# Front of a gated short-convolution layer: three of sixteen first sums on the matrix engine, a finer load, and three splits behind the front

## The chip, the cores and the metric

The kernel runs on one core of a Trainium2 chip. The core's engines work beside each other, each through its own list of instructions in a fixed order: TensorE (PE, matrix products; PEld is its loading of weights), VectorE (DVE), ScalarE (ACT), GpSimd (POOL) and SyncE (SP), which here issues nearly all transfers from the chip's memory. The metric is the device time of one execution in microseconds (us); lower is better.

## The reference, cut to what matters

One layer: a root-mean-square norm of x (256 tokens of 2048 features), a modulation whose shift, scale and gate come from a vector c through `ada_w` (2048 x 6144), a projection by `w_in` (2048 x 16384) into four quarters of 4096, a causal convolution of width 3 and two gatings, a projection back by `w_out` (4096 x 2048), the gated residual and a last norm, all in float32.

```python
h = rmsnorm(x, norm_g)
mod = einsum('bd,df->bf', silu(c), ada_w) + ada_b
shift, scale, gate = split(mod, 3)
h = h * (1.0 + scale) + shift
b_gate, c_gate, v, g = split(einsum('bsd,de->bse', h, w_in), 4)
u = causal_depthwise_conv(c_gate * v, conv_w)
y = einsum('bse,ed->bsd', b_gate * u * silu(g), w_out)
out = rmsnorm(x + gate * y, final_g)
```

## The kernel before, in words

**Products.** A float32 product is made of three faster ones: each weight tile is split into a rounded part `hi` (ScalarE, line 338) and the rest `lo` (VectorE, line 339), h likewise into `hh_` and `hl_`, and TensorE adds hi·hh, hi·hl and lo·hh (line 466). The raw weight tiles (`raw0`, `raw_s`) rotate through three buffers, `hi` and `lo` through three each.

**The front** (lines 195 to 403) is written out by hand, and `in_order` keeps it in that order on every engine. SyncE loads x, then the columns of `ada_w` for the first two 128-feature blocks of shift and scale (tiles `at0`, the k-th holding rows k of the 16 blocks of 128 rows), then the first weights `raw0`. The tiles `at0` borrow the buffers of `lo` and `hi` in turn, three of each. The first sums, silu(c) times these columns over the 16 blocks k, are made in two ways: for the k in `ON_PE` TensorE multiplies the columns directly (`sum0_of`, line 350); for the others VectorE accumulates into `gv0` (lines 362 and 364), and at the end TensorE adds up `gv0` over the partitions into the same bank (line 387). From the sums come `scale` and `shift`, and `features(k)` (lines 326 to 332) gives `hh_` on ScalarE and `hl_` on VectorE for the first two blocks k = 0, 1. Between these, TensorE turns x in four steps (`turn_x`, line 306) once ScalarE has scaled it (`scaled_x`), and makes idle products (`idle`, line 253), whose numbers stand in `IDLE`.

**Behind the front** a planner (`plan`) lays out steps: a step is a pair of chunks (of 512 columns each), a quarter, and a range of blocks k for which h is ready. The first steps have the two blocks k = 0, 1 alone: 24 products from `raw0`, 24 from a half load `raw_s`, then 48 for every whole load. Between the loads go pieces of the next modulation sums (`ada_piece`: two transfers of 256 KB to a tile `at`, four buffers; VectorE adds them into `gv`, lines 446 and 448). When a pair of blocks is summed, TensorE turns the sums (`tp_g`, line 455), ScalarE adds them up, and `features` gives the next two blocks of h. What lies behind the front is put in order by a scheduler that fills each engine's list with what it thinks ready, so a waiting instruction of the front can be passed by later work; on the engine itself the list is then followed strictly. Later stages (`mm_b`, line 466 too, and the projection back, lines 670 to 672) are not touched.

Of the kernel before, what the change touches and what calls it, by code (L numbers as in the profile page):

```python
# [11 lines left out]
ALU = mybir.AluOpType  # L12
# [116 lines left out]
def short_conv_layer(ctx: ExitStack, tc: tile.TileContext, x, c, norm_g, ada_w, ada_b, w_in, conv_w, w_out, final_g, out):  # L129
    nc = tc.nc  # L130
# [59 lines left out]
    ended = {}  # L190
# [5 lines left out]
    rows2 = const.tile([96, P], F32, tag="rows2", name="rows2")  # L196
    HX = D // 2
    GIVE = 300
    IDLE = (20, 8, 28, 2, 6, 4, 12, 8)
    xt = [[slot([P, HX], f"x{t}{dh}") for dh in range(2)] for t in range(TT)]  # L200
    for t in range(TT):
        for dh in range(2):
# [8 lines left out]
    adas = ada_w[0].rearrange("(k p) (s f) -> p k s f", p=P, s=3)  # L211
    NK0 = ADA[0]
    first_ada = []
    for n, (j, kk) in enumerate(((0, 4), (4, 4), (8, 4), (12, 2), (14, 1), (15, 1))):
        at = wpool.tile([P, SLOT], F32, tag=("lo", "hi")[n % 2], name="at0", bufs=3)[:, : kk * 2 * NK0 * P]
        at = at.rearrange("p (k s f) -> p k s f", k=kk, s=2)
        if n == 0:
            wpool.tile([P, 32], F32, tag="line3", name="line3", bufs=1)
        for s in range(2):
            nc.sync.dma_start(at[:, :, s, :], adas[:, j : j + kk, s, 0 : NK0 * P])  # L220
        first_ada.extend(at[:, i] for i in range(kk))
# [118 lines left out]
        return hi, lo  # L340


    ON_PE = (3, 7, 11, 13)
    sums0 = psum.tile([P, 512], F32, tag="sm", name="sum0", bufs=2)
    gv0 = adap.tile([P, 2, 2 * P], F32, tag="gv", name="gv0")[:, :, 0 : NK0 * P]

# [19 lines left out]
    scaled_x(1)  # L366
    turn_x(turned[0], 0)
    nc.scalar.copy(xs[0], turned[0])
    sum0_of(0)
    scaled_x(2)  # L370
    turn_x(turned[1], 1)
    nc.scalar.copy(xs[1], turned[1])
    idle(3, turned[2])
    sum0_of(1)
    idle(4, turned[2])
    scaled_x(3)
    turn_x(turned[2], 2)
    nc.scalar.copy(xs[2], turned[2])
    turned.append(psum.tile([P, CT, T], F32, tag="mm", name="tp_x"))
    idle(5, turned[3])  # L380
    sum0_of(2)
    turn_x(turned[3], 3)
    nc.scalar.copy(xs[3], turned[3])
    sum0_of(3)
    tp_idle = psum.tile([P, CT, T], F32, tag="mm", name="tp_idle")
    idle(6, tp_idle)
    sum0(None, gv0, ones[:, 0:1])

    sums_shift, sums_scale = sums0[:, 0:NK0], sums0[:, NK0 : 2 * NK0]
    ks = slice(0, NK0)  # L390
    nc.vector.tensor_tensor(out=scale[:, ks], in0=sums_scale, in1=b_scale1[:, ks], op=ALU.add)
    nc.vector.tensor_tensor(out=scale[:, ks], in0=scale[:, ks], in1=gT[:, ks], op=ALU.mult)
    nc.vector.tensor_tensor(out=shift[:, ks], in0=sums_shift, in1=b_shift[:, ks], op=ALU.add)
    hi0 = wpool.tile([P, SLOT], F32R, tag="hi", name="hi", bufs=3)
    lo0 = wpool.tile([P, SLOT], F32R, tag="lo", name="lo", bufs=3)
    w = CT * P
# [2 lines left out]
    for k in range(NK0):  # L399
        c = slice(k * w, (k + 1) * w)  # L400
        nc.vector.tensor_tensor(out=lo0[:, c], in0=raw0[:, c], in1=hi0[:, c].bitcast(F32), op=ALU.subtract)
        features(k)
    idle(7, tp_idle)
    pinned.close()
    pieces0 = [(hi0, lo0)]

# [87 lines left out]
    def keep(ch, q, k0, bank, seed=False):  # L494
# [4 lines left out]
        else:  # L499
            nc.vector.tensor_tensor(out=acc[ch, q], in0=bank, in1=acc[ch, q], op=ALU.add)  # L500

    def parts(chs, q, k0, k1, seeds, between):

        w = len(chs) * CT * P
# [16 lines left out]
        for s0, some in zip(range(k0, k1, step), between):  # L521
            sk = min(step, k1 - s0)
            n = sk * w
            raw = raw_tile("raw_s")
            nc.sync.dma_start(
                raw[:, :n].rearrange("p (k f) -> p k f", k=sk),
                w_in[0, s0 * P : (s0 + sk) * P, col : col + w].rearrange("(k p) f -> p k f", p=P),
            )
            hi, lo = split(raw, n)
            for piece in some:  # L530
                ada_piece(*piece)
            for j, (bank, seed) in enumerate(zip(banks, seeds)):
                if first == 0:
                    opening_products(bank, hi, lo, w, j * CT * P, s0, sk, k1)
                else:
                    for i in range(sk):
                        chunk_products(bank, hi, lo, i * w + j * CT * P, s0 + i, first, k1, seed)
# [236 lines left out]
```

## Time and profile before

| | |
|---|---|
| median of three runs | 913.68 us (913.65 to 915.89) |
| the profiled execution | 913.47 us, its span 911.7 us |
| TensorE busy in the span | 898.6 us (99%) |
| VectorE, ScalarE busy | 628.8 us (69%), 451.7 us (50%) |
| read from memory | 224.49 MB |

A row of the timeline gives the start, the duration, the engine (with q: its issuing part), the line, the operation, what is written and read, how many such instructions follow each other, and in brackets how long the engine sat idle before and what ended that. 913.47 less 911.7 leaves 1.8 us around the span, which is taken as fixed.

### The profile page before, as it was taken

Reading aid. Unit: us, or ns where it says so; the run is one execution under the profiler, and the core shown is the slowest. Engines: PE = TensorE matmul, PEld = TensorE weight load, DVE = VectorE, ACT = ScalarE, POOL = GpSimd, SP = SyncE. Lnnn points to the kernel's source line nnn. Section 1 sums busy time; section 2 is a strip of 40 time slices with the busy share of each in tenths; the row PEclk is TensorE's granted clock in tenths of the full one; section 3 lists DMA queues with packets and bytes.
Section 4 is the critical chain, followed back from the end, with each engine's and each line's share of the span. In section 5 each row is a group of like instructions: output and inputs, shape, how many; then the busy total and the mean of one; then the engine's idle time right before and its main releaser. Section 6 shows DMA issues by size and latency. Waiting matters only on the chain.

```text
span 911.7 us, 16332 instructions
## 1 busy us (share of the span) xinstructions
PE 898.6 (99%) x7111; PEld 866.5 (95%) x7111; DVE 628.8 (69%) x605; ACT 451.7 (50%) x427; POOL 0.7 (0%) x6
## 2 busy tenths in 40 slices
PE   8999999999999999999999999999999999999997
PEld 7899999999999999999999999999999988888885
DVE  4888989999988999985555455545455544555882
ACT  6678876544545755554333443334433333443333
POOL 0000000000000000000000000000000000000000
PEclk9999999999999999999999999999999999999999
DMA  9999999999898778867666666666666496665542
GB/s 305 375 384 372 321 361 349 329 362 351 286 350 308 239 246 280 281 225 223 198 188 187 193 200 202 190 186 191 200 192 201 141 346 213 198 202 195 185 139 92
DMA packets 146791, 227.64 MB, mean 250 GB/s; under 512 B 5360, under 2 KB 103840, under 8 KB 146336
## 3 DMA queue, kind: packets, MB, share of 16 engines
q1 hardware_dynamic: 146480, 226.51, 74.0%
q8 instruction: 55, 0.90, 0.4%
q14 instruction: 16, 0.13, 0.0%
q10 hardware_dynamic: 240, 0.09, 0.0%
HBM read 224.49 MB, written 2.10 MB: 249 GB/s over the span
## 4 chain that ended last, share of the span: by engine, by line
PE 95%; DMA 3%; DVE 1%; ACT 0%; SPq 0%; issue 0%; ACTq 0%; DVEq 0%
PE mm_b L466 38%; PE mm_s L466 37%; PE mm_o L671 6%; PE mm_o L670 6%; PE mm_o L672 6%; DMA raw_s<-in_sc_w_in_dram 1%; DMA at<-in_ada_w_dram 1%; DMA x<-in_x_dram 1%; DVE gv L364 1%; PE tp_g L455 0%; ACT hi L338 0%; PE ps_gate L609 0%; SPq L220 0%; DVE lo L339 0%; PE sum L350 0%; SPq L203 0%
## 5 line engine op out<-in xcount | busy, mean ns | idle before, releaser
L466 PE MATMUL mm_b<-hT,hi 128*128 128x256 f32 x2048 | 348.4, 276 | 0.0
L466 PE MATMUL mm_s<-hT,hi 128*128 128x256 f32 x2048 | 336.6, 277 | 1.6 <-ACT hi L338 1.0
L466 PEld LDWEIGHTS mm_b<-hT,hi 128*128 128x128 f32 x2048 | 308.4, 188 | 0.0
L466 PEld LDWEIGHTS mm_s<-hT,hi 128*128 128x128 f32 x2048 | 299.4, 188 | 2.5 <-ACT hi L338 1.2
L466 PE MATMUL mm_b<-hT,lo 128*128 128x256 f32 x1024 | 282.6, 276 | 0.0
L466 PE MATMUL mm_s<-hT,lo 128*128 128x256 f32 x1024 | 262.1, 276 | 0.0
L339 DVE TENSOR_TENSOR lo<-raw,hi 128x2048 fp32r<-128x2048 f32 x64 | 146.7, 2291 | 128.2 <-ACT hi L338 128.2
L338 ACT CAST hi<-raw 128x2048 fp32r<-128x2048 f32 x64 | 122.5, 1913 | 196.3 <-PE mm_b L466 149.0
L466 PEld LDWEIGHTS mm_b<-hT,lo 128*128 128x128 f32 x1024 | 192.2, 188 | 0.1
L466 PEld LDWEIGHTS mm_s<-hT,lo 128*128 128x128 f32 x1024 | 182.8, 188 | 0.0
L338 ACT CAST hi<-raw_s 128x2048 fp32r<-128x2048 f32 (+1 forms) x64 | 121.4, 1901 | 96.6 <-PE mm_s L466 79.5
L339 DVE TENSOR_TENSOR lo<-raw_s,hi 128x2048 fp32r<-128x2048 f32 (+1 forms) x64 | 145.4, 2272 | 21.2 <-ACT hi L338 20.1
L339 DVE TENSOR_TENSOR lo<-raw_o,hi 128x2048 fp32r<-128x2048 f32 x32 | 73.3, 2290 | 64.0 <-ACT hi L338 64.0
L338 ACT CAST hi<-raw_o 128x2048 fp32r<-128x2048 f32 x32 | 61.0, 1907 | 106.7 <-PE mm_o L672 81.3
L671 PE MATMUL mm_o<-lo,y 128*128 128x512 f32 x256 | 99.3, 389 | 0.0
L672 PE MATMUL mm_o<-hi,y 128*128 128x512 f32 x256 | 99.3, 389 | 0.0
L670 PE MATMUL mm_o<-hi,y 128*128 128x512 f32 x256 | 99.3, 389 | 0.0
L448 DVE SCALAR_TENSOR_TENSOR gv<-at,silu_c,gv 128x512 f32<-128x512 f32 x105 | 78.6, 749 | 2.1 <-DMA at<-in_ada_w_dram 0.3
L672 PEld LDWEIGHTS mm_o<-hi,y 128*128 128x128 f32 x256 | 48.0, 188 | 10.0
L670 PEld LDWEIGHTS mm_o<-hi,y 128*128 128x128 f32 x256 | 48.0, 188 | 10.0
L671 PEld LDWEIGHTS mm_o<-lo,y 128*128 128x128 f32 x256 | 48.1, 188 | 9.8
L498 ACT COPY acc<-mm_s 128x1024 f32<-128x1024 f32 x43 | 43.4, 1017 | 22.7 <-PE mm_s L466 22.3
(105 smaller groups left out, 386.8 us busy)
## 6 DMA issues: line engine op xcount, KB each, us to landing
raw<-in_sc_w_in_dram SPq DMA_DIRECT2D x64, 1024.0 KB, 5.6
raw_s<-in_sc_w_in_dram SPq DMA_DIRECT2D x63, 1024.0 KB, 7.2
raw_o<-in_sc_w_out_dram SPq DMA_DIRECT2D x32, 1024.0 KB, 5.2
at<-in_ada_w_dram SPq DMA_DIRECT2D x114, 256.0 KB, 7.4
at_g<-in_ada_w_dram SPq DMA_DIRECT2D x32, 512.0 KB, 6.2
at<-in_ada_w_dram SPq DMA_DIRECT2D x6, 512.0 KB, 8.7
x<-in_x_dram SPq DMA_DIRECT2D x4, 512.0 KB, 6.3
big<-in_x_dram SPq DMA_DIRECT2D x2, 1024.0 KB, 7.7
```

Of the source, the lines that this page charges most:

```text
L338: nc.scalar.copy(hi[:, :n], raw[:, :n])
L339: nc.vector.tensor_tensor(out=lo[:, :n], in0=raw[:, :n], in1=hi[:, :n].bitcast(F32), op=ALU.subtract)
L364: nc.vector.scalar_tensor_tensor(out=gv0, in0=first_ada[k], scalar=c_k, in1=gv0, op0=ALU.mult, op1=ALU.add)
L448: nc.vector.scalar_tensor_tensor(out=gv, in0=at4[:, i], scalar=c_k, in1=gv, op0=ALU.mult, op1=ALU.add)
L466: mm = last_mm[0] = nc.tensor.matmul(dst, w, h[:, k], start=begins and left, stop=ends, skip_group_check=True)
L498: nc.scalar.copy(acc[ch, q], bank)
L670: nc.tensor.matmul(po, yh, hi[:, o], start=opens, stop=False, skip_group_check=True)
L671: nc.tensor.matmul(po, yh, lo[:, o], start=False, stop=False, skip_group_check=True)
L672: nc.tensor.matmul(po, yl, hi[:, o], start=False, stop=ct == NCT - 1, skip_group_check=True)
```

## The change

It does five things:
- `ON_PE` is (7, 11, 13) and no longer (3, 7, 11, 13): k = 3 goes to VectorE.
- The third `at0` load of four blocks becomes two of two, so there are seven tiles `at0` for six borrowed buffers.
- The order on TensorE and ScalarE in the front changes, and `IDLE` with it: idle products stand on both sides of each of the last two direct sums.
- `scale` for each of the two blocks is one VectorE instruction of one column; `shift` stands between them.
- The splits of the first three `raw_s` loads are put behind the front's last instruction on their engines (`behind(ended)`).

```diff
-    IDLE = (20, 8, 28, 2, 6, 4, 12, 8)
+    IDLE = (20, 8, 30, 4, 3, 4, 8, 9, 9)
...
-    for n, (j, kk) in enumerate(((0, 4), (4, 4), (8, 4), (12, 2), (14, 1), (15, 1))):
+    for n, (j, kk) in enumerate(((0, 4), (4, 4), (8, 2), (10, 2), (12, 2), (14, 1), (15, 1))):
...
-    ON_PE = (3, 7, 11, 13)
+    ON_PE = (7, 11, 13)
...
-    sum0_of(0)
     scaled_x(2)
     turn_x(turned[1], 1)
+    idle(3, turned[2])
+    sum0_of(0)
+    scaled_x(3)
     nc.scalar.copy(xs[1], turned[1])
-    idle(3, turned[2])
-    sum0_of(1)
-    idle(4, turned[2])
-    scaled_x(3)
     turn_x(turned[2], 2)
     nc.scalar.copy(xs[2], turned[2])
     turned.append(psum.tile([P, CT, T], F32, tag="mm", name="tp_x"))
-    idle(5, turned[3])
-    sum0_of(2)
+    idle(4, turned[3])
     turn_x(turned[3], 3)
     nc.scalar.copy(xs[3], turned[3])
-    sum0_of(3)
     tp_idle = psum.tile([P, CT, T], F32, tag="mm", name="tp_idle")
+    idle(5, tp_idle)
+    sum0_of(1)
     idle(6, tp_idle)
+    sum0_of(2)
+    idle(7, tp_idle)
     sum0(None, gv0, ones[:, 0:1])
 
-    sums_shift, sums_scale = sums0[:, 0:NK0], sums0[:, NK0 : 2 * NK0]
-    ks = slice(0, NK0)
-    nc.vector.tensor_tensor(out=scale[:, ks], in0=sums_scale, in1=b_scale1[:, ks], op=ALU.add)
-    nc.vector.tensor_tensor(out=scale[:, ks], in0=scale[:, ks], in1=gT[:, ks], op=ALU.mult)
-    nc.vector.tensor_tensor(out=shift[:, ks], in0=sums_shift, in1=b_shift[:, ks], op=ALU.add)
+    for k in range(NK0):
+        if k == 1:
+            nc.vector.tensor_tensor(out=shift[:, 0:NK0], in0=sums0[:, 0:NK0], in1=b_shift[:, 0:NK0], op=ALU.add)
+        nc.vector.tensor_scalar(
+            out=scale[:, k : k + 1], in0=sums0[:, NK0 + k : NK0 + k + 1], scalar1=b_scale1[:, k : k + 1],
+            scalar2=gT[:, k : k + 1], op0=ALU.add, op1=ALU.mult,
+        )
...
-    idle(7, tp_idle)
+    idle(8, tp_idle)
...
+    first_pieces = [None] * 3
...
-            hi, lo = split(raw, n)
+            with behind(ended if first_pieces else {}):
+                hi, lo = split(raw, n)
+            first_pieces[:] = first_pieces[1:]
```

What the change moves is seen in the engines' lists as built. SyncE's list in the front, behind the loads of x; tiles `at_` with a number are the borrowed `at0`, `at` alone are the pieces of the next modulation sums, `raw_115` and `raw_118` are `raw0`. Before:

```order
L220 DMA at_96<-in_ada_w_dram 128x4x256 x2
L220 DMA at_100<-in_ada_w_dram 128x4x256 x2
L220 DMA at_103<-in_ada_w_dram 128x4x256 x2
L220 DMA at_106<-in_ada_w_dram 128x2x256 x2
L220 DMA at_109<-in_ada_w_dram 128x256 x2
L220 DMA at_112<-in_ada_w_dram 128x256 x2
L188 DMA raw_115<-in_sc_w_in_dram 128x512 x2
L525 DMA raw_s<-in_sc_w_in_dram 128x2x512
L435 DMA at<-in_ada_w_dram 128x2x256 x2
L525 DMA raw_s<-in_sc_w_in_dram 128x2x1024
L435 DMA at<-in_ada_w_dram 128x2x256 x6
L525 DMA raw_s<-in_sc_w_in_dram 128x2x1024 x2
```

And in the changed kernel, at the same place:

```order
L220 DMA at_96<-in_ada_w_dram 128x4x256 x2
L220 DMA at_100<-in_ada_w_dram 128x4x256 x2
L220 DMA at_103<-in_ada_w_dram 128x2x256 x2
L220 DMA at_106<-in_ada_w_dram 128x2x256 x2
L220 DMA at_109<-in_ada_w_dram 128x2x256 x2
L220 DMA at_112<-in_ada_w_dram 128x256 x2
L437 DMA at<-in_ada_w_dram 128x2x256 x8
L220 DMA at_115<-in_ada_w_dram 128x256 x2
L188 DMA raw_118<-in_sc_w_in_dram 128x512 x2
L529 DMA raw_s<-in_sc_w_in_dram 128x2x512
L529 DMA raw_s<-in_sc_w_in_dram 128x2x1024 x3
L437 DMA at<-in_ada_w_dram 128x2x256 x2
```

The seventh tile, `at_115` (k = 15), takes the buffer of `at_96`; its transfer stands behind eight transfers of the next sums' pieces, and `raw0` and all `raw_s` behind it. The waits in that list, at the turn, show why (DMAHW0 to 7 are eight counters, used in turn, each set by one transfer's landing; DVE is VectorE's):

```order
L437 DMA at<-in_ada_w_dram 128x2x256 [waits DMAHW2_49]
L437 DMA at<-in_ada_w_dram 128x2x256 [waits DMAHW3_49]
L220 DMA at_115<-in_ada_w_dram 128x256 [waits DMAHW4_49,DVE_49]
L220 DMA at_115<-in_ada_w_dram 128x256 [waits DMAHW5_49]
L188 DMA raw_118<-in_sc_w_in_dram 128x512 [waits DMAHW6_49]
```

Only `at_115` waits for VectorE, the reader of `at_96`; every transfer waits for the landing of the one issued eight before it.

VectorE's list from the end of the sums (`sum`) on, `xs` being the turned x and `hT` the parts of h; before, and then after:

```order
L391 TENSOR_TENSOR scale<-sum_221,b_scale_162 128x2
L392 TENSOR_TENSOR scale<-scale,vec 128x2
L393 TENSOR_TENSOR shift<-sum_221,vec 128x2
L401 TENSOR_TENSOR lo<-raw_115,hi 128x512
L339 TENSOR_TENSOR lo<-raw_s,hi 128x1024
L329 TENSOR_SCALAR xs_215<-xs_215,scale,shift 128x256
L332 TENSOR_TENSOR hT<-xs_215,hT 128x256
```

```order
L392 TENSOR_SCALAR scale<-sum_226,b_scale_165,vec 128x1
L391 TENSOR_TENSOR shift<-sum_226,vec 128x2
L392 TENSOR_SCALAR scale<-sum_226,b_scale_165,vec 128x1
L403 TENSOR_TENSOR lo<-raw_118,hi 128x512
L329 TENSOR_SCALAR xs_220<-xs_220,scale,shift 128x256
L332 TENSOR_TENSOR hT<-xs_220,hT 128x256
L403 TENSOR_TENSOR lo<-raw_118,hi 128x512
```

The split of the half load `raw_s` (128x1024) has moved from ahead of `hl_` of block 0 to behind the front; on ScalarE its `hi` has moved likewise, from ahead of `hh_` to behind it.

Later on VectorE, from behind the addition to `acc` (line 500, now 502) to `hl_` of block k = 4, before and after:

```order
L339 TENSOR_TENSOR lo<-raw_s,hi 128x2048
L448 SCALAR_TENSOR_TENSOR gv<-at,silu_c,gv 128x512
L339 TENSOR_TENSOR lo<-raw_s,hi 128x2048
L448 SCALAR_TENSOR_TENSOR gv<-at,silu_c,gv 128x512
L320 TENSOR_TENSOR scale<-gs,b_scale_162 128x2
L448 SCALAR_TENSOR_TENSOR gv<-at,silu_c,gv 128x512
L321 TENSOR_TENSOR scale<-scale,vec 128x2
L448 SCALAR_TENSOR_TENSOR gv<-at,silu_c,gv 128x512 x2
L329 TENSOR_SCALAR xs_216<-xs_216,scale,shift 128x256
L448 SCALAR_TENSOR_TENSOR gv<-at,silu_c,gv 128x512
L329 TENSOR_SCALAR xs_216<-xs_216,scale,shift 128x256
L332 TENSOR_TENSOR hT<-xs_216,hT 128x256
```

```order
L450 SCALAR_TENSOR_TENSOR gv<-at,silu_c,gv 128x512 x2
L339 TENSOR_TENSOR lo<-raw_s,hi 128x2048
L320 TENSOR_TENSOR scale<-gs,b_scale_165 128x2
L450 SCALAR_TENSOR_TENSOR gv<-at,silu_c,gv 128x512
L321 TENSOR_TENSOR scale<-scale,vec 128x2
L450 SCALAR_TENSOR_TENSOR gv<-at,silu_c,gv 128x512 x3
L339 TENSOR_TENSOR lo<-raw_s,hi 128x2048
L329 TENSOR_SCALAR xs_221<-xs_221,scale,shift 128x256
L450 SCALAR_TENSOR_TENSOR gv<-at,silu_c,gv 128x512
L329 TENSOR_SCALAR xs_221<-xs_221,scale,shift 128x256
L332 TENSOR_TENSOR hT<-xs_221,hT 128x256
```

Seven additions to `gv` stand there now instead of six, beside the same two `lo`. Ahead of this `hl_`, counted from the end of the front, VectorE's list holds 43 additions to `gv` and 14 whole `lo` instead of 40 and 13.

## The prediction, on record before the changed kernel ran

> **What bounds the kernel now.** I read the page first, then the waits of TensorE, then the timeline of the first 42 us.
>
> ```profile
> PE 898.6 (99%) x7111; PEld 866.5 (95%) x7111; DVE 628.8 (69%) x605; ACT 451.7 (50%) x427; POOL 0.7 (0%) x6
> ```
>
> TensorE is busy 99% of the span. Its waits from 26.5 us to the end are three:
>
> ```profile
> PE mm_s L466 <- ACT hi L338: 1.0, 1, 1.0
> PE mm_s L466 <- ACT hT L328: 0.4, 1, 0.4
> PE mm_s L466 <- DVE hT L332: 0.2, 1, 0.2
> ```
>
> All three lie before 40 us, and from there the products follow each other to the last stage. So time is won or lost here: when the first product starts, how long the next ones wait, and whether a new wait opens later. The timeline of the front:
>
> ```profile
> 13.54 0.49 DVE L362 TENSOR_SCALAR gv<-at,silu_c 128x512 f32<-128x512 f32 x1 [0.80 <-DMA at<-in_ada_w_dram]
> 14.06 1.54 DVE L364 SCALAR_TENSOR_TENSOR gv<-at,silu_c,gv 128x512 f32<-128x512 f32 x2
> 16.55 2.33 DVE L364 SCALAR_TENSOR_TENSOR gv<-at,silu_c,gv 128x512 f32<-128x512 f32 x3 [0.95 <-DMA at<-in_ada_w_dram]
> 19.58 4.69 DVE L364 SCALAR_TENSOR_TENSOR gv<-at,silu_c,gv 128x512 f32<-128x512 f32 x6 [0.70 <-DMA at<-in_ada_w_dram]
> 22.43 1.67 PE L253 MATMUL tp_idle<-ones_r 128*128 128x256 f32 x12
> 23.18 1.20 ACT L398 CAST hi<-raw 128x512 fp32r<-128x512 f32 x2 [0.35 <-DMA raw<-in_sc_w_in_dram]
> 24.32 1.05 PE L350 MATMUL sum<-ones,gv 128*128 128x1 f32 x8 [0.22 <-DVE gv L364]
> 25.24 1.19 PE L253 MATMUL tp_idle<-ones_r 128*128 128x256 f32 x8
> 25.26 1.05 ACT L338 CAST hi<-raw_s 128x1024 fp32r<-128x1024 f32 x1 [0.88 <-DMA at<-in_ada_w_dram]
> 25.41 0.16 DVE L391 TENSOR_TENSOR scale<-sum,b_scale 128x2 f32<-128x2 f32 x1 [1.15 <-PE sum L350]
> 25.68 0.15 DVE L393 TENSOR_TENSOR shift<-sum,vec 128x2 f32<-128x2 f32 x1
> 26.22 1.09 ACT L328 ACTIVATE hT<-xs,shift,scale 128x256 fp32r<-128x256 f32 x2
> 26.86 0.74 PE L466 MATMUL mm_s<-hT,hi 128*128 128x256 f32 x4 [0.44 <-ACT hT L328]
> ```
>
> VectorE waits three times for an arriving 1 MB of `ada_w` columns, at 13.54, 16.55 and 19.58, so 1 MB lands every 3.02 us and 256 KB every 0.755 us: the transfers run back to back. The last addition ends at 24.27 and everything up to the first product at 26.86 hangs on it.
>
> **The change, part by part.**
>
> *k = 3 to VectorE* adds one addition of 0.78 us (4.69 / 6). The two additions before it end at 15.60 and the next data come at 16.55: it lies in that wait and costs nothing. *The finer load* lets k = 8 start when k = 6 ends, at 18.88 instead of 19.58. That would gain 0.7 us if k = 15 were there; it is not.
>
> *The seventh tile.* The list of SyncE puts `at_115` behind eight transfers of 256 KB. Without them k = 15 lands with the fourth MB, at 19.58 + 3.02 = 22.60; from the other side, `raw0`, whose first 256 KB land next, is there at 23.18, so 23.18 - 0.755 = 22.42. Eight times 0.755 is 6.04 us: k = 15 starts between 28.46 and 28.64, I take **28.55** instead of the last addition's 24.27 - 0.76 = 23.51. That is 5.04 us later. The rest of the first sums is long done by then.
>
> *From the last addition to the first product.* Before: sums on TensorE 24.32, first product 26.86, so 2.54 us, and ScalarE was in the way: its `hi` of `raw_s` ran until 26.31 while shift was ready at 25.83. Now that `hi` stands behind, and shift is VectorE's second instruction instead of the third. The sums start at 29.35 and are done 1.05 later; 0.04 to VectorE (25.41 - 25.37), two instructions 0.22, 0.04 to ScalarE: 30.70. `raw0` lands two steps of 0.755 behind k = 15, so its two casts (1.20) end near 30.6 and just fit. From the start of `hh_` to the first product 0.64 (26.86 - 26.22): **31.4**, so 4.55 us later than before. The nine idle products, from 30.27 at 0.12 each, end there too.
>
> *Waits that go.* After the first product two waits stood:
>
> ```profile
> 27.91 0.28 PE L466 MATMUL mm_s<-hT,hi 128*128 128x256 f32 x1
> 28.41 0.85 PE L466 MATMUL mm_s<-hT,hi 128*128 128x256 f32 x5 [0.22 <-DVE hT L332]
> 27.59 1.93 SPq L525 DMA_DIRECT2D raw_s<-in_sc_w_in_dram  x2
> 37.58 1.90 ACT L338 CAST hi<-raw_s 128x2048 fp32r<-128x2048 f32 x1 [3.41 <-DMA raw_s<-in_sc_w_in_dram]
> 39.53 0.74 PE L466 MATMUL mm_s<-hT,hi 128*128 128x256 f32 x4 [0.98 <-ACT hi L338]
> ```
>
> The first was `hl_` behind the `lo` of `raw_s`, 0.4 us between starts; that `lo` now stands behind. The second was the second whole load: issued at 27.59 behind a late buffer, landed at 37.5, and TensorE waited 1.0 to 1.2 us. Now the pieces of the next sums came earlier, and this load is issued when `raw0` is split (about 33), with only one load in flight. Where one or two are in flight, a whole load takes 5.6 us from issue to landing, and half of `raw0` took 4.7:
>
> ```profile
> raw<-in_sc_w_in_dram SPq DMA_DIRECT2D x64, 1024.0 KB, 5.6
> raw<-in_sc_w_in_dram SPq DMA_DIRECT2D x2, 256.0 KB, 4.7
> ```
>
> So it lands near 38.6 and its `hi` is there at 40.5. TensorE needs it after 96 products, 11.1 us behind the first (39.53 - 26.86 - 1.5), at 42.5. Both waits go, 1.2 us by the view of waits and 1.6 by starts; I take 1.5. Net so far: 4.55 - 1.5 = **+3.05**.
>
> *The rest of TensorE.* Idle products kept it going until 24.1 before. Now it has done its last one at about 24.5 (a direct sum of 0.95 less, six more idle products, the data of k = 13 there at 19.58 + 1.51 = 21.1), and k = 15 lets it go on only at 29.35: a rest of 4.8 us, which the trace of before shows nowhere in its middle. Rows that bound it:
>
> ```profile
> 4.41 4.52 PE L253 MATMUL tp_x<-ones_r 128*128 128x256 f32 x20
> 10.15 3.60 PE L253 MATMUL tp_x<-ones_r 128*128 128x256 f32 x28
> 4.40:8.40 4.00, 4.00 (x19) 4.00 (x19) 0.00 (x0) 3.83 (x7) 0.00 (x0) 1.00 0.99 326
> ```
>
> The same idle product takes 0.22 us in the first row, behind a rest of at least 4.2 us, and 0.125 in the second: TensorE starts slow and goes to full pace after 4.2 us. After the rest of 0.98 at 39.53 it was not slow. 4.8 us is nearer to the rest that was, so I take the slow start. Then the eight sum products take 1.65 instead of 0.92, and the nine idle ones 1.93; those end at 29.35 + 1.65 + 1.93 + 0.1 = 33.05, behind which the first product waits: 1.65 later than 31.4. Half a us more at slow pace up to 29.35 + 4.2 costs 0.2. So **+1.85**, bounded by 0 and, if the slow stretch is half as long again, 2.9. The Trainium skill, "TensorE: Matmul & The Clock Gate", Part 1, says that one idle window of about 3.4 us halves the clock and one busy window restores it; the windows run freely. By that rule a rest of 4.8 us holds a whole window in about four cases in ten, and then the price is the same, otherwise nothing; the 4.2 us above agree with it. The clock column (third row, the window from 4.4 to 8.4) reads 1.00 over the slow products, so here it can't decide.
>
> *A wait later.* `hl_` of block k = 4 was on its edge:
>
> ```profile
> 89.72 1.23 DVE L500 TENSOR_TENSOR acc<-mm_s,acc 128x1024 f32<-128x1024 f32 x1 [1.09 <-PE mm_s L466]
> 100.26 0.42 DVE L332 TENSOR_TENSOR hT<-xs,hT 128x256 fp32r<-128x256 f32 x1
> 100.40 0.72 PE L466 MATMUL mm_s<-hT,hi 128*128 128x256 f32 x3
> ```
>
> It ended at 100.68; the second product of k = 4 wanted it at 100.51. The chain starts with the addition to `acc`, which TensorE releases, and now has seven additions to `gv` in place of six: 0.78 later, so **+0.8** on TensorE. But VectorE must come to that `acc` on time. What it does between shift and the next sums:
>
> ```profile
> 26.35 1.22 DVE L339 TENSOR_TENSOR lo<-raw_s,hi 128x1024 fp32r<-128x1024 f32 x1
> 28.27 0.68 DVE L401 TENSOR_TENSOR lo<-raw,hi 128x512 fp32r<-128x512 f32 x1
> 28.88 0.41 DVE L329 TENSOR_SCALAR xs<-xs,scale,shift 128x256 f32<-128x256 f32 x1
> 29.32 0.42 DVE L332 TENSOR_TENSOR hT<-xs,hT 128x256 fp32r<-128x256 f32 x1
> 29.66 0.48 DVE L446 TENSOR_SCALAR gv<-at,silu_c 128x512 f32<-128x512 f32 x1
> ```
>
> Now that is 30.65 + 2 (0.68 + 0.41 + 0.42) + 1.22 = 34.9 instead of 29.66, 5.2 us later (6 with the slow start), and ahead of `acc` stand 3.9 us more (two additions and a `lo`, the third addition being the one counted); TensorE comes 3 to 5 later. The balance, 4 to 6 us, must come out of VectorE's waits from 29.6 to 90:
>
> ```profile
> DVE lo L339 <- ACT hi L338: 6.6, 4, 2.7
> DVE shift L322 <- ACT tp_g L457: 1.5, 1, 1.5
> DVE acc L500 <- PE mm_s L466: 1.1, 1, 1.1
> ```
>
> 9.2 us: enough. Features of later blocks came ten us ahead of their products; I count nothing for them.
>
> Sum: 913.47 + 3.05 + 1.85 + 0.8 = **919.2 us**. The median shown, 913.68, is 0.2 above the profiled execution; the range takes that in.
>
> **The rivals.**
>
> *A. The same delay, TensorE keeps its pace* (the rest breaks no pace, or ends sooner): 913.47 + 3.05 + 0.8 = 917.3, and 916.5 if the later wait has slack too. For it: no slowing after any rest in this trace up to 0.98. Against it: 4.8 is far from 0.98.
>
> *B. k = 15 does not wait for its place; not slower by more than 0.3%.* If the sixteen DMA engines serve the small transfer beside the eight larger ones, it lands 4.7 us after its issue, as `raw0` did. It is issued when the first of the eight lands, 22.5 + 0.1, the second half one step later: 23.4 + 4.7 = 28.1 at worst, 27.3 for the first half. At 27.3 the first product comes 1.25 earlier and the rest shrinks to 3.6: 913.47 + 1.8 + 0.8 = 916.1. It decides from there: every us before 28.55 is a us. Against it: 3.02 us per MB three times over show transfers landing in turn.
>
> *C. The change does what its lines say*, k = 15 in its written place: last addition ends at 23.4, first product near 25.5, but the whole load at 37.5 stays and takes back most: 912.6 to 913.5. Against it: the list.
>
> *D. VectorE is late at k = 4*: one more wait for `hi` of 2.7 (the longest above), with the slow start: 919.2 + 1.9 = 921.1.
>
> **How the numbers follow.** Forecast 0.45, A 0.32, B 0.09, C 0.04, D 0.10. The range from 915.9 to 921.2 holds forecast, A, most of B and D. About 0.3%, 2.74 us, is what a measurement of this kernel can tell from no change: slower lies above 916.2. Forecast, A and D lie there: slower 0.86 (A's lower end is close to it); B and C give same 0.12; faster 0.02, as nothing behind the front can shorten.
>
> **What would show it.** `raw0`'s first cast near 29.3 instead of 23.18; the last addition to `gv` near 28.5 with a wait of some 5 us on a transfer; a rest on TensorE before the sums; idle products behind it at 0.21 (forecast) or 0.12 (A); no wait at the 96th product; a wait of about 1 us at the first products of k = 4. If the last addition starts at 23 the step on the queue is wrong, and with it nearly all of this.

## The result, and the profile after

The changed kernel takes **919.83 us** (median of 6 runs, 919.37 to 920.68), the kernel before 913.86 beside it (913.55 to 915.89): ratio 1.0062, 95% interval 1.0049 to 1.0075. It is slower by 0.6%, 0.6 us above the predicted 919.2 and inside the range. The profiled execution took 920.21 us with a span of 918.4, which is 6.74 us more than the 913.47 of before.

The timeline of the changed kernel, at the places that the prediction named (start and duration in us, engine, line, what, and in brackets the idle time ahead and what ended it):

```profile
22.69 1.32 PE L253 MATMUL tp_idle<-ones_r 128*128 128x256 f32 x9
29.30 0.75 DVE L364 SCALAR_TENSOR_TENSOR gv<-at,silu_c,gv 128x512 f32<-128x512 f32 x1 [6.66 <-DMA at<-in_ada_w_dram]
29.94 1.20 ACT L400 CAST hi<-raw 128x512 fp32r<-128x512 f32 x2 [8.73 <-DMA raw<-in_sc_w_in_dram]
30.10 1.87 PE L350 MATMUL sum<-ones,gv 128*128 128x1 f32 x8 [6.10 <-DVE gv L364]
31.83 2.27 PE L253 MATMUL tp_idle<-ones_r 128*128 128x256 f32 x9
33.90 1.05 PE L468 MATMUL mm_s<-hT,hi 128*128 128x256 f32 x4
...
45.30 1.86 PE L468 MATMUL mm_s<-hT,hi 128*128 128x256 f32 x15
```

The addition of k = 15 starts at 29.30 instead of 23.51, having waited 6.66 us for a transfer; TensorE rests 6.1 us ahead of the sums; the eight sums (1.87 us) and the nine idle products behind them (2.27) take 0.23 and 0.25 us each, where the rows of before give 0.13 and 0.15; the first product of the main work starts at 33.90 instead of 26.86. The last row is the 96th product's place (here and below products are counted along TensorE from 0): 45.30 instead of 39.53, with no wait in brackets. TensorE's waits from 28 us to the end are now these two:

```profile
PE sum L350 <- DVE gv L364: 6.1, 1, 6.1
PE mm_s L468 <- DVE acc L502: 0.9, 1, 0.9
```

The three waits of before are gone. The second one is new, and stands far behind the front:

```profile
326.84 1.23 DVE L502 TENSOR_TENSOR acc<-mm_s,acc 128x1024 f32<-128x1024 f32 x1
328.12 0.50 PE L468 MATMUL mm_s<-hT,hi 128*128 128x256 f32 x2 [0.91 <-DVE acc L502]
```

The granted clock of TensorE changes in this trace only at steps of 3.41 us. The view by windows, cut at those steps (PE's and the other engines' busy us with the instructions started, then the granted clock, the DMA share and GB/s):

```profile
24.69:28.10 3.41, 0.00 (x0) 0.00 (x0) 0.00 (x0) 0.00 (x0) 0.00 (x0) 1.00 1.09 349
28.10:31.51 3.41, 1.41 (x7) 1.41 (x7) 0.75 (x1) 1.20 (x2) 0.00 (x0) 0.50 0.96 364
31.51:34.93 3.42, 3.42 (x17) 3.42 (x17) 2.85 (x9) 2.48 (x4) 0.00 (x0) 0.50 0.31 125
34.93:38.34 3.41, 3.41 (x32) 3.41 (x31) 3.37 (x5) 1.69 (x2) 0.00 (x0) 1.00 0.75 239
```

One window passes with nothing on TensorE; the next two are granted half the clock; the one after is full again.

The whole difference can be followed by the place of a product on TensorE's list, after minus before: first product +7.04, 96th +5.77, 640th +5.39, 2000th +5.38, 2560th +6.63, 3500th +6.63 us. So the loss is made ahead of the 96th product (5.8), a little comes back (0.4), and 1.2 us are added between the 2400th and the 2560th.

### The profile page after: what moved, and what is told of

It reads as the page before. It is cut to its first block, busy times and chain, and to the rows that moved or that the text cites. A ratio compares the mean times of both kernels' runs of the same rounds, so it can differ in the third digit from the quotient of the medians.

```text
span 918.4 us, 16340 instructions
## 1 busy us (share of the span) xinstructions
PE 900.1 (98%) x7110; PEld 868.2 (95%) x7110; DVE 628.8 (68%) x606; ACT 451.9 (49%) x427; POOL 0.7 (0%) x6
## 4 chain that ended last, share of the span: by engine, by line
PE 90%; DMA 4%; DVE 4%; issue 1%; ACT 0%; SPq 0%; ACTq 0%; DVEq 0%
PE mm_b L468 38%; PE mm_s L468 32%; PE mm_o L676 6%; PE mm_o L677 6%; PE mm_o L678 6%; DMA at<-in_ada_w_dram 2%; DMA at_g<-in_ada_w_dram 2%; DVE lo L339 1%; DVE gacc L608 1%; DMA x<-in_x_dram 1%; DVE acc L502 0%; DVE acc L412 0%; PE tp_g L457 0%; DVE acc L415 0%; PE tp_idle L253 0%
```

## The experiments

**The two theories.** *Queue*: k = 15 stands behind eight transfers on SyncE's list; the late landing, the rest of TensorE with its half pace, and a later list on VectorE all follow. *Edits*: the direct sums, idle products, splits behind the front, or the seventh tile's wait for its buffer cost time by themselves. The kernel before was measured beside each run (medians 913.75 to 913.81). What the expectations call the planner's list is the order that the scheduler gives each engine.

**Six tiles again, all else as changed.**

```diff
-    for n, (j, kk) in enumerate(((0, 4), (4, 4), (8, 2), (10, 2), (12, 2), (14, 1), (15, 1))):
+    for n, (j, kk) in enumerate(((0, 4), (4, 4), (8, 4), (12, 2), (14, 1), (15, 1))):
```

> The changed kernel with the front's ada_w again in six tiles instead of seven, all else as changed (three sums on TensorE, the nine idle products, the splits behind the front). SyncE's list then has k = 15 ahead of the eight transfers, as before the change.
> Theory (k = 15 queued behind eight transfers is the cause; the rest of TensorE and the later list follow from it): the last addition to gv starts at 23.5 us, TensorE rests less than 1.5 us ahead of the sums and its idle products behind them take 0.12 us each, the first product starts at 26.0 to 26.9, the wait of about 1 us at the 96th product (for the second whole load) is back, the wait near 328 us is gone. Median 912.6 to 914.2, within 0.1% of the kernel before.
> Rival (the other edits cost time by themselves: three direct sums, the splits put behind, idle products): first product later than 27.5 although k = 15 comes at 23.5, median over 915.

Measured: 914.91 us (913.43 to 915.39, 11 runs), ratio 1.0004, interval 0.9995 to 1.0012. The first product starts at 26.47, and the wait near 328 us is gone. What the theory lacked stands at the 96th product, in the timeline and the windows:

```profile
37.85 1.90 ACT L338 CAST hi<-raw_s 128x2048 fp32r<-128x2048 f32 x1
39.80 2.44 PE L468 MATMUL mm_s<-hT,hi 128*128 128x256 f32 x13 [1.99 <-ACT hi L338]
```

```profile
37.27:40.68 3.41, 1.42 (x12) 1.22 (x12) 2.08 (x3) 3.41 (x4) 0.00 (x0) 1.00 1.06 386
40.68:44.10 3.42, 3.42 (x18) 3.42 (x18) 3.42 (x3) 1.78 (x1) 0.00 (x0) 0.50 1.06 364
44.10:47.51 3.41, 3.41 (x32) 3.41 (x31) 3.01 (x4) 1.22 (x2) 0.00 (x0) 1.00 1.08 371
```

TensorE comes to the 96th product earlier, waits 2.0 us instead of 1.0 for the same load, and that rest brings a window of half pace (18 products instead of 32), some 1.6 us. The median lies 0.7 above the theory's upper end. Of the 11 executions the five with a granted clock of 0.998 or more took 913.43 to 914.23 us, the six with 0.997 took 914.91 to 915.39. Only one execution of each kernel has a trace; that the group with the lower clock is the one with the window of half pace is an inference, here and below. (The kernel before has such a group too, 0.6 us slower in the median, and there it can come from the kernel's end, where the clock is halved too: 0.50 from 909.76 us in its trace.) So the other edits together show neither a gain nor a loss by the interval, though the median is 1.1 above the kernel before.

**The finer load alone**, in the kernel before.

```diff
-    for n, (j, kk) in enumerate(((0, 4), (4, 4), (8, 4), (12, 2), (14, 1), (15, 1))):
+    for n, (j, kk) in enumerate(((0, 4), (4, 4), (8, 2), (10, 2), (12, 2), (14, 1), (15, 1))):
```

> The kernel before with one edit: the front's ada_w in seven tiles instead of six. The four direct sums, the idle products and the splits in the front stay.
> Theory (the place of k = 15 on SyncE's queue is the cause): this alone gives the whole loss; the last addition to gv starts near 29.3 us, TensorE rests 4 to 6 us and then runs at half pace, the first product starts at 33 to 34.5, the additions to gacc stand earlier on VectorE's list and a wait of about 1 us opens near 328 us. Median 918.5 to 920.5.
> Rival (the loss needs the other edits too): median under 917.

Measured: 919.76 us (918.27 to 920.69, 5 runs), ratio 1.0061, interval 1.0048 to 1.0074: the whole loss, from one line. The timeline:

```profile
28.32 0.75 DVE L364 SCALAR_TENSOR_TENSOR gv<-at,silu_c,gv 128x512 f32<-128x512 f32 x1 [5.98 <-DMA at<-in_ada_w_dram]
...
29.13 1.87 PE L350 MATMUL sum<-ones,gv 128*128 128x1 f32 x8 [5.51 <-DVE gv L364]
```

The first product starts at 32.71, 0.3 earlier than expected. The direct sums, the idle products and the splits fall as the cause; the seventh tile's wait for its buffer is still in this kernel, and the run with k = 15 in its place settles it.

The wait near 328 us does not show in this execution (918.27, the quickest of the five; the other four took 919.43 to 920.69). Yet VectorE's list is the same there: as many additions to `gacc` (the sums of the gate, made from pieces `at_g` of `ada_w`) stand ahead of the additions to `acc`. What differs is how long VectorE sits for one such piece, here and in the changed kernel:

```profile
293.96 2.33 DVE L602 SCALAR_TENSOR_TENSOR gacc<-at_g,silu_c,gacc 128x512 f32<-128x512 f32 x3 [1.92 <-DMA at_g<-in_ada_w_dram]
296.76 2.33 DVE L608 SCALAR_TENSOR_TENSOR gacc<-at_g,silu_c,gacc 128x512 f32<-128x512 f32 x3 [3.72 <-DMA at_g<-in_ada_w_dram]
```

The piece landed 6.1 us after its issue here and 8.0 us in the changed kernel. So, by these two executions, the list opens the door to that wait, and a late landing makes it.

**The rest filled.**

```diff
-    IDLE = (20, 8, 30, 4, 3, 4, 8, 9, 9)
+    IDLE = (20, 8, 30, 4, 3, 4, 8, 52, 9)
```

> The changed kernel with 52 idle products instead of 9 between the third direct sum and the last sums, which keep TensorE going while it waits for k = 15. Nothing else differs but what the planner moves for it.
> Theory (TensorE runs at half pace for a while behind a rest of 6 us, which costs 1.9 to 2.2 us): the granted clock stays at 1.00 from 10 to 40 us, the idle products behind the sums take 0.12 us each instead of 0.21 to 0.25, the sums 0.12 instead of 0.21, the first product starts at 31.7 to 32.3 instead of 33.9, limited by hT. Median 1.6 to 2.4 us under the changed kernel, 917.4 to 918.2.
> Rival (the half pace is hidden anyway, hT comes no earlier): first product later than 33.3, difference under 0.7 us. If the idle products run past 29.9 us, the sums start later by as much, and that is to be taken off.

Measured: 922.95 us (921.92 to 923.61, 4 runs), ratio 1.0093, interval 1.0078 to 1.0109: slower, where the theory had 917.4 to 918.2. At the front it did what was expected:

```profile
30.09 1.05 PE L350 MATMUL sum<-ones,gv 128*128 128x1 f32 x8 [0.40 <-DVE gv L364]
...
32.27 0.74 PE L468 MATMUL mm_s<-hT,hi 128*128 128x256 f32 x4
```

The sums take 1.05 us instead of 1.87, the first product starts 1.63 us earlier than 33.90, and the clock is 1.00 from 10 us on. The 384th product is still 1.64 us ahead of the changed kernel, the 640th 0.5, the 2560th 3.4 behind. TensorE's waits say where it went:

```profile
PE mm_s L468 <- DVE acc L502: 2.6, 1, 2.6
PE mm_s L468 <- ACT mm_s L516: 1.1, 2, 0.5
PE mm_s L468 <- DVE lo L339: 0.5, 2, 0.3
```

So the half pace is real and costs 1.6 us at the front; and the scheduler, for which TensorE's time had moved, wrote another list behind it.

**k = 15 in its place, seven tiles kept.** The first later group of `ada_w` is put behind the front.

```diff
-        for s in range(2):
-            nc.sync.dma_start(at4[:, :, s, :], adas[:, j : j + kk, s, k0 * P : k0 * P + w])
+        with behind(ended if k0 == NK0 else {}):
+            for s in range(2):
+                nc.sync.dma_start(at4[:, :, s, :], adas[:, j : j + kk, s, k0 * P : k0 * P + w])
```

> The changed kernel with seven tiles, in which the first later group of ada_w transfers is put behind the front (as the splits are): SyncE's list then has k = 15 straight behind k = 14. The tile of k = 15 still takes a buffer that an earlier tile of the front must give up, as in the changed kernel.
> Theory (the eight transfers ahead cost, not the wait for the buffer): k = 15 lands near 22.5, the last addition to gv starts at 22.4 to 23.6 us, no rest over 2 us on TensorE, first product at 25.0 to 26.5. The second whole load is issued behind late buffers as before, and the 96th product waits for it: median 911.5 to 914, not slower than the kernel before.
> Rival (the wait for the buffer delays k = 15): last addition later than 26 us, median over 916.

Measured: 915.53 us (913.02 to 916.71, 11 runs), ratio 1.0013, interval 1.0004 to 1.0022. The timeline:

```profile
23.38 0.75 DVE L364 SCALAR_TENSOR_TENSOR gv<-at,silu_c,gv 128x512 f32<-128x512 f32 x1 [0.49 <-DMA at<-in_ada_w_dram]
...
26.37 0.72 PE L469 MATMUL mm_s<-hT,hi 128*128 128x256 f32 x4
...
40.45 1.85 PE L469 MATMUL mm_s<-hT,hi 128*128 128x256 f32 x13 [1.96 <-ACT hi L338]
```

The tile of k = 15 still needs the buffer of an earlier one, and is on time: the eight transfers ahead cost the 6 us, not that wait. The time is 1.5 above the theory's upper end, again by the 96th product: a wait of 1.96, and half pace behind it. The four executions at 0.998 or more took 913.02 to 914.03, the seven below 915.34 to 916.71. The seventh tile's wait for its buffer falls as the cause.

**The gate sums put back.** In the changed kernel each addition to `gacc` gets an order behind the sum (addition to `acc`) that stood ahead of it before.

```diff
-            nc.vector.tensor_tensor(out=acc[ch, q], in0=bank, in1=acc[ch, q], op=ALU.add)
+            added.append(nc.vector.tensor_tensor(out=acc[ch, q], in0=bank, in1=acc[ch, q], op=ALU.add).ins.name)
...
+            for n, first in ((5, 5), (6, 15), (7, 29), (9, 40), (11, 43), (13, 53)):
+                if gated[0] >= first and len(added) > n:
+                    tc.add_manual_dep(g.ins, added[n], after, reason="behind a sum")
+            gated[0] += 1
```

> The changed kernel, in which the additions of the gate sums (gacc) are put back, on VectorE's list, behind the sums they stood behind before the change: 5 instead of 11 ahead of the sixth addition to acc, 40 instead of 47 ahead of the tenth, and so on. The front stays as changed.
> Theory (the wait of 0.9 us near 328 us comes from seven additions of 0.75 us that the planner's list moved ahead): the front is as in the changed kernel (first product near 33.9 us, late), TensorE's wait for acc near 328 us is gone, median 918.2 to 919.2, some 1 us under the changed kernel.
> Rival (that wait comes from transfers or from TensorE itself): a wait of 0.5 us or more remains between 300 and 335 us, median over 919.5.

Measured: 919.14 us (918.87 to 920.60, 5 runs), ratio 1.0063, interval 1.0049 to 1.0077. The median is 0.7 under the changed kernel's, in two sets of runs whose intervals lie over each other; the trace is what tells. From 20 us to the end it has one wait left:

```profile
PE sum L350 <- DVE gv L364: 5.7, 1, 5.7
```

The profiled executions differ by 1.34 us, of which 1.2 arise between the 2400th and 2560th product. The product that waited, the 2544th, starts at 326.93 here and at 328.12 in the changed kernel. There, and with the finer load alone, it stands behind the addition to `acc` on VectorE; here, as in the kernel before, it has only ScalarE to wait for, which is done in time.

**Rest filled and gate sums put back.**

> Both edits together: 52 idle products in the rest of the front, and the additions of the gate sums put back as they stood before.
> Theory (the idle products did win 1.6 us at the front, and a later list took more back): the half pace is gone and the first product starts near 32.3, the wait of 2.6 us near 330 us is gone, and the median falls by 2.6 to 3.6 us against the run with the idle products alone, to 919.3 to 920.3. The 1.1 us of waits between 90 and 106 us, which came with the idle products too, remain; without them it would be 918.
> Rival (the list is not it): a wait of over 1 us near 330 us, median over 922.

The edits are the two above. Measured: 919.44 us (918.05 to 920.04, 6 runs), ratio 1.0057, interval 1.0044 to 1.0071: 3.5 us under the run with the idle products alone, as expected, so that list was the cause there too. But the half pace was not gone in the profiled execution:

```profile
27.98:31.39 3.41, 2.21 (x19) 2.01 (x19) 0.75 (x1) 1.19 (x2) 0.00 (x0) 1.00 0.96 338
31.39:34.81 3.42, 3.42 (x18) 3.42 (x18) 3.29 (x10) 2.24 (x5) 0.00 (x0) 0.50 0.45 178
```

The window ahead held a rest of 1.2 us and eight sums of one column (1.05 us). Three executions at 0.997 took 919.99 to 920.04, three at 0.998 took 918.05 to 918.90: 1.1 to 2 us apart, about the price of one window, in the same kernel.

**Two pieces held back.** As the run with k = 15 in its place, and the last two pieces of that group are issued behind the second whole load.

```diff
+                if k0 == NK0 and floor[0]:
+                    tc.add_manual_dep(at_dma.ins, floor[0], after, reason="behind a load")
...
+            loads[0] += 1
+            if loads[0] == 3:
+                floor[0] = raw_dma.ins.name
+                for piece in held:
+                    ada_piece(*piece)
             for piece in some:
-                ada_piece(*piece)
+                if loads[0] < 3 and piece[0] == NK0 and piece[2] >= 2:
+                    held.append(piece)
+                else:
+                    ada_piece(*piece)
```

> Seven tiles and all other edits of the change, with k = 15 straight behind k = 14 on SyncE's queue (the first later group of ada_w behind the front), and of that group's four pieces the last two put behind the second whole load instead of ahead of it.
> Theory (with k = 15 in its place the next limit is the second whole load, which lands behind 2 MB of ada_w; 1 MB of it moved behind, it lands 3 us earlier): first product at 26.4, hi of the second whole load ends near 36.8 instead of 40.4, no wait of over 0.3 us at the 96th product, no half pace behind it; the 96th product starts at 37.4 to 38 instead of 39.5 in the kernel before. Median 911.3 to 912.5, 1.2 to 2.4 us under the kernel before.
> Rival (what is put off is missed later): the features of the next blocks come 3 us later, and a wait of 1 us or more opens before 110 us; median 913.3 or more.

Measured: **912.52 us** (911.51 to 913.55, 11 runs), ratio 0.9987, interval 0.9979 to 0.9996: a little under the kernel before. The `hi` of the second whole load runs from 34.59 to 36.51, and the 96th product does not wait. But TensorE was at half pace at another place, so the first product came at 27.33, 0.9 later than expected:

```profile
21.94:25.35 3.41, 3.13 (x28) 2.92 (x26) 1.50 (x2) 1.11 (x2) 0.00 (x0) 1.00 1.05 358
25.35:28.77 3.42, 3.42 (x17) 3.42 (x18) 3.22 (x10) 2.13 (x4) 0.00 (x0) 0.50 1.01 387
```

The window ahead was busy for 3.13 of 3.41 us. Of that, 1.8 us were products with one column (eight of a direct sum, eight of the last sums).

**The splits behind the front alone**, in the kernel before.

```diff
-            hi, lo = split(raw, n)
+            with behind(ended if first_pieces else {}):
+                hi, lo = split(raw, n)
+            first_pieces[:] = first_pieces[1:]
```

> The kernel before with one edit: the splits of the first three loads (raw_s) behind the front. Six tiles, four direct sums, the idle products of before.
> Theory (this edit saves 0.4 us between the first products and gives it back at the 96th product, which waits for the second whole load): first product at 26.2 to 26.9, the wait of 0.4 for the second product gone, the 96th product at 39.5 to 39.9. Median within 0.1% of the kernel before, 913.0 to 914.7. Where the wait ahead of the 96th product exceeds 1.5 us, a stretch of half pace may follow and cost up to 1.7.
> Rival (the edit itself costs): 96th product later than 40.5 or median over 915.5.

Measured: 915.00 us (913.42 to 915.99, 11 runs), ratio 1.0009, interval 1.0000 to 1.0017, 0.3 above the theory's upper end. First product at 26.77, the second product's wait gone, and at the 96th:

```profile
39.92 4.04 PE L466 MATMUL mm_s<-hT,hi 128*128 128x256 f32 x32 [1.99 <-ACT hi L338]
```

```profile
34.94:38.36 3.42, 2.99 (x27) 2.79 (x25) 3.28 (x5) 1.30 (x2) 0.00 (x0) 1.00 1.02 401
38.36:41.77 3.41, 1.85 (x15) 1.85 (x16) 2.10 (x2) 3.41 (x3) 0.00 (x0) 1.00 1.06 387
41.77:45.18 3.41, 3.41 (x31) 3.41 (x30) 3.41 (x4) 1.07 (x2) 0.00 (x0) 1.00 1.06 360
```

What it saves ahead, it waits longer there. In this execution the wait of 2 us lies across two windows and no half pace follows; six of the eleven, at 0.997 or less, took 915.00 to 915.99, the five above 913.42 to 914.57.

**Two pieces held back, third direct sum on VectorE.**

```diff
-    ON_PE = (7, 11, 13)
+    ON_PE = (7, 11)
-    IDLE = (20, 8, 30, 4, 3, 4, 8, 9, 9)
+    IDLE = (20, 8, 30, 4, 3, 4, 8, 17, 9)
```

> As the run with the two pieces held back (seven tiles, k = 15 in its place, the last two pieces of the next group behind the second whole load), but the third direct sum (k = 13) goes to VectorE too, and 17 idle products instead of 9 stand ahead of the last sums.
> Theory (products of one column count little for the clock: the direct sum and the last sums, 2 us of products of one column in a window of 3.41 us, brought the half pace from 25.35 to 28.77 us in that run; VectorE has 0.87 us of waiting there for one addition more): the granted clock stays at 1.00 from 20 to 60 us, first product at 26.3 to 26.6, 96th product at 37.2 to 37.8; the hT of the next block, which came 0.6 us late at 73.0 us, may be late by up to 2 now. All executions at a granted clock of 0.998 or more, median 911.0 to 912.0.
> Rival (the half pace came from something else, or VectorE is late by the addition): half pace in the profile or in some executions, or first product over 27, median 912.4 or more.

Measured: 913.93 us (913.48 to 916.23, 11 runs), ratio 1.0004, interval 0.9995 to 1.0013: missed by 2 us. The front is as the theory has it (clock 1.00 from 20 to 60 us, first product 26.66, VectorE on time), the 96th product at 38.21, 0.4 later than expected. Then a wait that no run had before:

```profile
101.51 0.38 PE L471 MATMUL mm_s<-hT,lo 128*128 128x256 f32 x1 [1.92 <-DVE lo L339]
```

VectorE's list had changed again: a `lo` is late at 101.5, and half pace follows from 103.03.

**One piece held back**, else as the last.

> The same, but only the last of the four pieces is held back behind the second whole load (0.5 MB, not 1 MB).
> Theory (each 256 KB of ada_w ahead of the second whole load costs that load 0.75 us, and each behind it comes later for the next block): hi of the second whole load ends near 38.3, the 96th product waits 0.5 to 1 us for it, the wait for hT near 73 us falls to 0 to 0.5. Median 911.3 to 912.5.
> Rival: wait for hT at 73 us as long as with two pieces held, or the wait at the 96th product over 1.5 us; median 912.8 or more.

Measured: **912.55 us** (912.13 to 913.23, 11 runs), ratio 0.9986, interval 0.9977 to 0.9995, at the theory's upper end. First product 26.61, the 96th at 37.59 with no wait (its `hi` ended at 36.70, earlier than the theory's 38.3), full clock to the last stage, and one wait behind the front, no shorter than with two pieces held:

```profile
71.64 3.12 PE L471 MATMUL mm_s<-hT,hi 128*128 128x256 f32 x25 [0.55 <-DVE hT L332]
```

With the run that holds two pieces back it is the best version found: both lie 1.2 us under the kernel before, 7.3 under the changed one, and their medians cannot be told apart.

**Idle products of one column**, in the kernel before: the twelve ahead of the last sums.

```diff
+            if n == 6:
+                nc.tensor.matmul(where[:, 0, 0:1], ones, ones[:, 0:1], start=True, stop=True, skip_group_check=True)
+            else:
+                nc.tensor.matmul(where[:, 0, :], ones_r[:, 0:P], ones_r[:, T:], start=True, stop=True, skip_group_check=True)
```

> The kernel before with one edit: the twelve idle products ahead of the last sums have one column (as the products of the sums) instead of 256. They take about the same time on TensorE by the rows (0.12 us each), so TensorE is as busy as before by its instructions. The planner moves some later instructions for it, so its median says little.
> Theory (a window of 3.41 us sets the next one to half pace where too few columns go through TensorE in it, whatever its instructions' busy time): the granted clock falls to 0.50 for 3.41 us at some time between 22 and 29 us in the profile or in most of the executions (granted clock of 0.997 or less), as it did not before, and the first product starts 0.3 to 1.7 us later than 26.86.
> Rival (only a rest counts, not the columns): granted clock 1.00 from 10 to 60 us, first product at 26.7 to 27.1, executions at 0.998 or more as often as before.

Measured: 917.19 us (915.67 to 918.26, 10 runs), ratio 1.0033, interval 1.0024 to 1.0042; all ten executions at a granted clock of 0.992 to 0.995. The timeline and the windows:

```profile
22.27 4.66 PE L254 MATMUL tp_idle<-ones 128*128 128x1 f32 x24
26.80 1.84 PE L353 MATMUL sum<-ones,gv 128*128 128x1 f32 x8
```

```profile
22.93:26.34 3.41, 3.41 (x18) 3.41 (x18) 1.25 (x2) 1.50 (x3) 0.00 (x0) 0.50 0.99 346
26.34:29.76 3.42, 3.42 (x17) 3.42 (x18) 1.04 (x5) 1.29 (x3) 0.00 (x0) 0.50 1.04 383
29.76:33.17 3.41, 3.41 (x18) 3.41 (x18) 3.38 (x6) 2.32 (x3) 0.00 (x0) 0.50 1.09 346
33.17:36.58 3.41, 3.41 (x32) 3.41 (x32) 3.34 (x5) 0.00 (x0) 0.00 (x0) 1.00 1.00 358
```

A miss in one respect: in this type twelve products are 24 instructions, which, at half pace, hold up the last sums to 26.80; the first product starts at 30.36, 3.5 us late where 0.3 to 1.7 were expected. But the question is answered: TensorE is busy without a gap, and at half clock for three windows, until one is full of wide products.

## Why the prediction came out as it did

The sum was 913.47 + 3.05 + 1.85 + 0.8 = 919.2, the profiled execution 920.21. By its steps:

- **k = 15 behind eight transfers: right.** Predicted start 28.55, measured 29.30, and 28.32 with the finer load alone. The run with k = 15 in its place shows that these transfers are the cause. The 0.98 us between these two arise at one place: the first of the eight transfers lands 1.78 us behind k = 14's last (21.49 to 23.27) in the changed kernel and 0.77 behind it (21.45 to 22.22) with the finer load alone; from there both go in steps of some 0.75. What holds that one transfer up is open.
- **From the last addition to the first product: right.** 2.05 us (29.35 to 31.4) were predicted at full pace; with the rest filled it was 2.18 (30.09 to 32.27).
- **The two waits that go: right.** From the 4th product to the 96th, 10.55 us instead of 12.09, that is 1.54 less; 1.5 was predicted.
- **The rest of TensorE and the slow start: right in kind, and in size.** The rest was 6.1 instead of 4.8, by the later landing and because the idle products ended at 24.0, not 24.5. From the sums to the first product 3.80 us (30.10 to 33.90) against a predicted 3.70 (29.35 to 33.05), and 1.63 less with the rest filled. Rival A, full pace, is refuted by the idle products' 0.25 us. The half pace behind the first product cost 0.3 more (+7.04 at the first, +7.31 at the 4th), where 0.2 was counted. The forecast had a slow start of 4.2 us behind the rest, up to 33.55, after the one at the program's beginning; the trace shows two windows of 3.41, up to 34.93, so the price fits, but the slow stretch has another cause and end.
- **`hl_` of block k = 4, +0.8: wrong.** The failed step is "now has seven additions to `gv` in place of six: 0.78 later, so +0.8 on TensorE". VectorE's part came true: from the addition to `acc` to the end of the `hT` it took 11.8 us,

```profile
95.37 1.23 DVE L502 TENSOR_TENSOR acc<-mm_s,acc 128x1024 f32<-128x1024 f32 x1 [0.25 <-PE mm_s L468]
...
106.77 0.42 DVE L332 TENSOR_TENSOR hT<-xs,hT 128x256 fp32r<-128x256 f32 x1
```

  against 10.96 before (89.72 to 100.68), 0.86 more. But the scheduler had moved TensorE's list too: the first product that needs it stood 626th before and stands 650th now, at 109.00, behind 107.19. At the 626th place, 106.28, it would have waited 0.9. No wait came, and the small one of before went. (That one was 0.1 us: the product that waited is the third of k = 4, at 100.73, not the second, as the prediction read it.)
- **What the sum did not have: the wait near 328 us, 1.2.** The scheduler put six additions to `gacc` more ahead of the eleventh addition to `acc` (48, where 42 stood); it comes at 326.84 where it came at 318.18, and TensorE's next bank is free only behind it. In this execution the piece that those additions wait for also landed late, as shown above. The run with the additions put back has no such wait. This term is about the size of the failed one, so in that part the total came out near by luck: without either, the sum would be 918.4 and the kernel near 919.

At the 96th product, up to where the argument reached, 4.9 us were predicted (4.55 + 1.85 - 1.5) and 5.77 measured; 0.75 of the difference is the landing.

**The rivals.** B (k = 15 not waiting for its place) is refuted by 29.30. C gave 912.6 to 913.5 for k = 15 in its written place; the run that puts it there took 913.02 to 914.03 in the executions with the higher clock, and 915.53 in the median: its price was near, but left out the half pace that follows the longer rest at the 96th product. D (VectorE late at k = 4) did not come.

## What to carry to other kernels

Where a transfer must wait for a buffer, read from the list what the scheduler issues in its stead: one more tile of 256 KB put the last and most urgent one behind 2 MB. A local edit in a scheduled kernel also rewrites the list far behind it, so compare whole lists by place, not only the edited stage; here it brought waits of 0.9, 2.6 and 1.9 us in three kernels, at places that none of the edits named. And where the front saves time, look at what the next product waits for: the second whole load took back what the splits behind the front had won, until ada_w pieces were moved behind it.

## What the runs showed of the hardware

A window of the clock need not be idle to halve the next one. Windows of 3.41 us with 1.42 and 1.52 us of wide products (128x256; the six tiles, and k = 15 in its place, whose row stands below) were followed by half pace; with 1.85 (the splits alone) and 2.2 (the rest filled, where 52 idle products end at 29.69 in the window from 27.48) they were not. The last stage of the run with the gate sums put back narrows it (its products have 512 columns; the third figure from the end is the clock):

```profile
38.56:41.97 3.41, 1.52 (x13) 1.52 (x14) 1.92 (x2) 3.41 (x4) 0.00 (x0) 1.00 1.05 387
41.97:45.39 3.42, 3.42 (x19) 3.42 (x18) 3.42 (x3) 1.15 (x1) 0.00 (x0) 0.50 1.07 361
...
908.56:911.97 3.41, 1.64 (x8) 1.02 (x6) 1.02 (x4) 2.03 (x5) 0.00 (x0) 1.00 0.75 308
911.97:915.38 3.41, 0.00 (x0) 0.00 (x0) 0.66 (x1) 0.85 (x2) 0.00 (x0) 1.00 0.70 287
```

The first pair is the run with k = 15 in its place, the second the last stage: 1.64 us were enough for full clock in the next window. All thirteen traces agree, from their first clock record on: every window with up to 1.53 us of products of 128 columns or more (each counted from its start to the next one's) was followed by half pace, every one with 1.64 or more by the full clock. So the bound lies a little under half a window.

Rests of 2.0 us were enough, where they fell into one window, and cost about 1.6 us more than themselves; in the run with the splits alone a rest of 1.99 us lay across two windows and cost nothing more. Where the windows lie differs from trace to trace, which would account for the 1 to 2 us by which the times of one kernel spread.

Products of one column count little towards it: 24 of them and eight sums filled TensorE's time from 22.27 to 28.6 us and got half the clock from 22.93 on. The busy share of the profile does not show this, only the granted clock does.

The Trainium skill, "TensorE: Matmul & The Clock Gate", Part 1, says that the clock is halved after an idle window of about 3.4 us and restored by a busy one, in windows that run freely. The windows' length, their free run and the restoring agree (3.41 us, and always one full window of wide products); the condition does not, as the windows of 1.42 and 1.52 us show. By the Trainium skill's condition the rest of 4.8 us that was predicted would have been harmless about six times in ten, an estimate from its 3.4 us; by the measured one a rest of that length leaves a window with at most 1.0 us of products wherever it falls ((6.83 - 4.8) / 2), so the slow start was no matter of luck.
